# Decoder step on one core: the up-projection's adding DMA is loaded with another weight part, and loads and splits are emitted in turn

## The chip, the core and the metric

The kernel runs on one core of a Trainium2 chip. A time is the device time of one execution in microseconds (us); the figure for a kernel is the median of its runs. A core has five engines with a queue each, which work in their program's order: TensorE (PE; its weight loads are listed as PEld), VectorE (DVE), ScalarE (ACT), GpSimd (POOL) and SyncE (SP). Here SP only issues DMA transfers; POOL issues the adding ones.

## The reference, cut to what matters

One layer of a hybrid decoder for 576 tokens (512 of a prompt, 64 of eight samples), all in float32, with a model width of 1024:

```python
xn = rms_norm(h, g_mix);  z = xn @ w_in                        # 1024 -> 6144
...                                                            # short convolution, pooling, gates
h = h + (gate_a * ya + gate_b * yb) @ w_o
hn = rms_norm(h, g_mlp)
h = h + jnp.square(jax.nn.relu(hn @ w_up)) @ w_down            # 1024 -> 4096 -> 1024
gp = jax.nn.sigmoid(rms_norm(h, g_ple) @ w_ple_gate)
h = h + gp * (p @ w_ple_proj);  y = rms_norm(h, g_final)
```

## The kernel before

Every float32 product is made of three matmuls on float32r parts: a number is split into hi (rounded) and lo (the rest), and hi·hi, hi·lo and lo·hi are added up. So every weight has to be split on the chip. A weight part is 128 x 512 numbers (256 KB). Its way is: SP loads it into one of the 8 buffers `raw` (line 114); ACT writes hi (line 79) and DVE writes lo (line 80) into one of the NF = 7 buffer pairs of `wsp`; PE uses it. A `raw` buffer comes free when the last reader of its part is through, a `wsp` pair when PE is through with it. A new part takes the `raw` buffer that has been free the longest, and its load waits on SP for that buffer's last reader, which is nearly always the lo of an earlier part on DVE.

The list `order` holds all parts in the order of use, and the class `Stream` emits loads and splits ahead of the use: `take` hands out parts and sees to it that splits are emitted up to NF parts beyond the oldest part in use, and loads some parts beyond that. A scheduler then orders each engine's instructions by its own estimates; a load or split emitted earlier does not have to run earlier.

The up-projection `w_up` is done in four blocks (`b`) of 1024 columns, each followed by its block of `w_down`. In a block the columns go in four pairs of 128-column units (`Pair`), and a pair takes seven products instead of eight (Strassen-Winograd: sums of quarter blocks of the weights times sums of quarter blocks of the activations). The weights of a pair are the quarters a, b (of the first unit) and c, d (of the second), and the forms to be multiplied are a, s2 = (c+d)+a, s0 = c+a (up to the signs of the algorithm), s1 = c+d, b, d and s3 = -s2-b:

```python
order += [Form(pairs[0], "a")]
for q in range(NQ):
    order += [Form(pairs[q], n) for n in ("s2", "s0", "s1", "b")]
    if q + 1 < NQ:
        order += [Form(pairs[q + 1], "a")]
    order += [Form(pairs[q], n) for n in ("d", "s3")]
```

Two of these sums are made by the DMA engines: `Pair.summed` loads c by SP and then has POOL issue a DMA from `w_up` that adds d (for s1) or a (for s0) onto the same `raw` tile (line 140); POOL waits for the plain load before it issues. s2 is made from s1's tile and a's tile by DVE (line 160, tile `s`), s3 by DVE too (line 162).

PE multiplies the forms in `quarter` (line 481), twelve matmuls a form. Products share four PSUM tiles `ab` and `cd`, and DVE combines them in between: line 532 (`u`, after the product for s2), line 534 (`g`, after that for s0), line 536 (after that for s1), line 557 at the pair's end. A product that is added onto such a tile waits until DVE has read it. These instructions stand in the same DVE queue as the splits and lines 160 and 162.

Of the kernel before, what the change touches and what calls it, by code (L numbers as in the profile page):

```python
# [42 lines left out]
def tile_hybrid_step(ctx: ExitStack, tc: tile.TileContext, x, pt, vecs, rc, ident, sconv, spool, w_first, w_in,  # L43
# [68 lines left out]
    def raw_tile(ap):  # L112
        raw = wraw.tile([P, KH], F32, tag="raw", name="raw")
        nc.sync.dma_start(raw, ap)
        return raw

    class Part:

        def __init__(self, ap, resident=False):
            self.ap, self.resident = ap, resident  # L120

        def load(self):
            self.raw = raw_tile(self.ap)
# [19 lines left out]
    class Form:  # L143
# [2 lines left out]

        def load(self):
            p, name = self.pair, self.name
            if name in ("a", "b", "d"):
                setattr(p, "r" + name, raw_tile(getattr(p, name)))  # L150
            elif name == "s2":
                p.rs1 = p.summed(p.c, p.d)
            elif name == "s0":
                p.rs0 = p.summed(p.c, p.a)

# [8 lines left out]
            return split(p.rs2 if name == "s3" else getattr(p, "r" + name), [P, KH], wsp, "w")  # L164

    class Stream:
        def __init__(self, items, loads=5):
            self.items, self.loads = items, loads
            self.nload, self.used, self.parts = 0, 0, []

        def fill(self, loads, splits):
            n = len(self.items)
            while self.nload < min(loads, n):
                self.items[self.nload].load()
                self.nload += 1
            while len(self.parts) < min(splits, n):
                self.parts.append(self.items[len(self.parts)].split())

        def take(self, n=1, live=0):

            first = self.used - live
            for i in range(n):
                splits = min(self.used + n + NF - 1, first + NF)
                self.fill(splits + self.loads, splits)
            out = self.parts[self.used:self.used + n]
            for i in range(self.used, self.used + n):
                self.parts[i] = self.items[i] = None
            self.used += n
            return out
# [165 lines left out]
    for j in range(NJ):  # L355
# [16 lines left out]
        n = CEXT - (CW - 1)  # L372
# [398 lines left out]
```

## Time and profile before

| | |
|---|---|
| median of 3 runs | 921.03 us (918.36 to 922.82) |
| the profiled execution | 923.7 us, of which 921.9 us are the span from the first to the last instruction |
| PE busy (matmul) | 898.6 us, 97% of the span |
| DVE, ACT, POOL busy | 521.3, 370.1, 113.4 us |
| weights and data | 89.60 MB read, 2.99 MB written |
| granted TensorE clock, mean | 0.984 of full speed |

PE is busy nearly throughout, so the time is PE's work, the stretches in which it waits, and the stretches in which it is granted half its clock. The blocks of `w_up` run at about 437 to 485 us, 535 to 586 us, 637 to 688 us and 739 to 791 us; they are called blocks 0 to 3.

### The profile page before, as it was taken

The numbers are of one execution on the slowest core, as the hardware profiler recorded it, in microseconds if no ns is written. First come the engines' busy times: TensorE is split into PE (matmuls) and PEld (weight loads), VectorE is DVE, ScalarE is ACT, GpSimd is POOL, SyncE is SP. The second block draws the span as 40 slices with busy tenths as digits, with TensorE's granted clock in tenths as the row PEclk, the third lists the DMA queues.
The fourth block names the chain that finished last, engine by engine and source line by source line (L and its number), as shares of the span: only waits on it lengthen the run. The fifth ranks groups of instructions, "written<-read, shape, count | busy, mean of one in ns | idle before, by whom it ended". The sixth has DMA issues, their size and how long they took to land.

```text
span 921.9 us, 16512 instructions
## 1 busy us (share of the span) xinstructions
PE 898.6 (97%) x6650; PEld 893.6 (97%) x6650; DVE 521.3 (57%) x832; ACT 370.1 (40%) x626; POOL 113.4 (12%) x150
## 2 busy tenths in 40 slices
PE   8999999999999999999999998999899989999995
PEld 7999999999999999999999998999899989999995
DVE  7654444433336687778863246544574356687555
ACT  8222222332113333355674245512472145545532
POOL 5000000000001221022100010010000010021243
PEclk9999999999999999999999999999899998999997
DMA  7422222222222222334544453363443453322102
GB/s 266 140 81 82 89 82 81 84 84 89 81 82 80 86 85 82 105 103 99 155 127 114 105 126 111 94 146 92 124 128 97 105 126 109 99 92 97 31 10 94
DMA packets 52653, 93.66 MB, mean 102 GB/s; under 512 B 6240, under 2 KB 9952, under 8 KB 52576
## 3 DMA queue, kind: packets, MB, share of 16 engines
q1 hardware_dynamic: 47824, 84.18, 28.8%
q0 software_dynamic: 4608, 8.39, 5.8%
q8 instruction: 52, 0.85, 0.4%
q14 instruction: 25, 0.20, 0.1%
q10 hardware_dynamic: 144, 0.03, 0.0%
HBM read 89.60 MB, written 2.99 MB: 100 GB/s over the span
## 4 chain that ended last, share of the span: by engine, by line
PE 92%; DMA 3%; ACT 2%; DVE 2%; issue 1%; POOL 0%; SPq 0%; DVEq 0%; POOLq 0%
PE ps L95 67%; PE cd L481 10%; PE ab L481 7%; PE psg L95 6%; DMA raw<-w_up 2%; PE psf L95 1%; PE psn L323 1%; DVE lo L80 1%; ACT hi L79 1%; ACT hi L82 0%; PE psn L307 0%; POOL sq L298 0%; ACT sq L294 0%; DMA xall<-x 0%; DVE xall L653 0%
## 5 line engine op out<-in xcount | busy, mean ns | idle before, releaser
L79 ACT CAST hi<-raw 128x512 fp32r<-128x512 f32 x290 | 177.8, 619 | 404.7 <-PE ps L95 325.9
L95 PE MATMUL ps<-hi,lo 128*128 128x288 f32 x1552 | 332.7, 296 | 0.0
L95 PE MATMUL ps<-lo,hi 128*128 128x288 f32 x1552 | 332.6, 296 | 0.0
L95 PE MATMUL ps<-hi 128*128 128x288 f32 x1552 | 332.5, 296 | 0.0
L80 DVE TENSOR_TENSOR lo<-raw,hi 128x512 fp32r<-128x512 f32 x290 | 203.7, 710 | 151.9 <-ACT hi L79 150.4
L95 PEld LDWEIGHTS ps<-hi,lo 128*128 128x128 f32 x1552 | 250.2, 189 | 0.0
L95 PEld LDWEIGHTS ps<-hi 128*128 128x128 f32 x1552 | 250.1, 189 | 0.0
L95 PEld LDWEIGHTS ps<-lo,hi 128*128 128x128 f32 x1552 | 250.1, 189 | 0.0
L481 PE MATMUL cd<-hi 128*128 128x288 f32 x256 | 78.2, 306 | 8.8 <-DVE g L534 8.6
L481 PE MATMUL cd<-lo,hi 128*128 128x288 f32 x256 | 77.0, 301 | 1.4 <-DVE lo L80 1.4
L481 PE MATMUL cd<-hi,lo 128*128 128x288 f32 x256 | 77.0, 301 | 0.0
L140 POOL DMA_DIRECT2D raw<-w_up x32 | 27.9, 879 | 330.8 <-DVE lo L80 154.0
L481 PEld LDWEIGHTS cd<-hi 128*128 128x128 f32 x256 | 49.1, 192 | 10.6 <-DVE g L534 9.4
L481 PE MATMUL ab<-hi 128*128 128x288 f32 x192 | 59.1, 308 | 0.0
L298 POOL TENSOR_TENSOR sq<-sq 128x576 f32<-128x576 f32 (+2 forms) x34 | 43.0, 1264 | 126.7 <-ACT sq L294 70.7
L481 PE MATMUL ab<-hi,lo 128*128 128x288 f32 x192 | 58.3, 305 | 0.0
L481 PE MATMUL ab<-lo,hi 128*128 128x288 f32 x192 | 58.1, 302 | 0.0
L481 PEld LDWEIGHTS cd<-lo,hi 128*128 128x128 f32 x256 | 49.4, 193 | 1.6 <-DVE lo L80 1.6
L481 PEld LDWEIGHTS cd<-hi,lo 128*128 128x128 f32 x256 | 49.4, 193 | 0.0
L481 PEld LDWEIGHTS ab<-hi 128*128 128x128 f32 x192 | 37.8, 197 | 1.5 <-ACT g L519 0.7
L95 PE MATMUL psg<-hi 128*128 128x320 f32 (+1 forms) x128 | 38.2, 298 | 0.0
L481 PEld LDWEIGHTS ab<-hi,lo 128*128 128x128 f32 x192 | 37.9, 198 | 0.0
(129 smaller groups left out, 882.4 us busy)
## 6 DMA issues: line engine op xcount, KB each, us to landing
raw<-w_in SPq DMA_DIRECT2D x90, 256.0 KB, 2.7
raw<-w_up SPq DMA_DIRECT2D x80, 256.0 KB, 2.9
raw<-w_down SPq DMA_DIRECT2D x64, 256.0 KB, 2.7
raw<-w_up POOLq DMA_DIRECT2D x32, 256.0 KB, 4.6
raw<-w_oc SPq DMA_DIRECT2D x16, 256.0 KB, 2.7
raw<-w_o SPq DMA_DIRECT2D x16, 256.0 KB, 2.7
raw<-w_pg SPq DMA_DIRECT2D x16, 256.0 KB, 2.8
xall<-x SPq DMA_DIRECT2D x7, 288.0 KB, 5.5
```

The source lines that it names most:

```text
L79: nc.scalar.copy(hi, src)
L80: nc.vector.tensor_tensor(out=lo, in0=src, in1=as32(hi), op=ALU.subtract)
L95: nc.tensor.matmul(o, wt, cols(at), start=start and i == 0, stop=stop and i == 2)
L140: nc.gpsimd.dma_start(raw, y, accum_op=ALU.add)
L298: nc.gpsimd.tensor_tensor(out=self.parts[0], in0=self.parts[0], in1=sq, op=ALU.add)
L323: nc.tensor.matmul(self.ps[:, h, c:c + m], self.y[:, i:i + 1].broadcast_to([m, P]), idt[:m, :m], start=True, stop=True)
L481: nc.tensor.matmul(o, wt, at, start=start and k == 0 and i == 0, stop=stop and k == NQ - 1 and i == 2, skip_group_check=True)
```

## The change

Three things are edited. The stream's number `loads` goes from 5 to 6. `fill` emits a load, a split, a load, a split, where it emitted all loads and then all splits of a call. And the tile of s1, with its plain load and its adding DMA, is loaded together with a of the same pair, where it was loaded with s2; in `order`, a stands three places ahead of s2 (one place in a block's first pair).

```diff
         def load(self):
             p, name = self.pair, self.name
+            if name == "a":
+                p.rs1 = p.summed(p.c, p.d)
             if name in ("a", "b", "d"):
                 setattr(p, "r" + name, raw_tile(getattr(p, name)))
-            elif name == "s2":
-                p.rs1 = p.summed(p.c, p.d)
             elif name == "s0":
                 p.rs0 = p.summed(p.c, p.a)
...
     class Stream:
-        def __init__(self, items, loads=5):
+        def __init__(self, items, loads=6):
...
         def fill(self, loads, splits):
             n = len(self.items)
-            while self.nload < min(loads, n):
-                self.items[self.nload].load()
-                self.nload += 1
+            def load(upto):
+                while self.nload < min(upto, n):
+                    self.items[self.nload].load()
+                    self.nload += 1
+
             while len(self.parts) < min(splits, n):
+                load(len(self.parts) + self.loads)
                 self.parts.append(self.items[len(self.parts)].split())
+            load(loads)
...
             for i in range(n):
                 splits = min(self.used + n + NF - 1, first + NF)
-                self.fill(splits + self.loads, splits)
+                self.fill(0, splits)
```

Lines below `fill` stand four lines further down in the changed kernel (line 534 is line 538 there). Three places show what moved in the programs.

The loads on SP for the third and fourth pair of block 1 (numbers are kept in the names here). Before, `raw_6104` is s1 of the third pair, `raw_6124` its s0, `raw_6162` its b, `raw_6194` a of the fourth pair, `raw_6214` d of the third, `raw_6252` s1 of the fourth, `raw_6272` s0 of the fourth:

```order
L114 DMA raw_6104<-w_up 128x512
L114 DMA raw_6124<-w_up 128x512
L114 DMA raw_6162<-w_up 128x512
L114 DMA raw_6194<-w_up 128x512
L114 DMA raw_6214<-w_up 128x512
L114 DMA raw_6252<-w_up 128x512
L114 DMA raw_6272<-w_up 128x512
```

Now `raw_6069` is d of the second pair, `raw_6124` s0 and `raw_6162` b of the third, and then `raw_6194` is s1 of the fourth, `raw_6197` its a, `raw_6217` d of the third, `raw_6272` s0 of the fourth:

```order
L114 DMA raw_6069<-w_up 128x512
L114 DMA raw_6124<-w_up 128x512
L114 DMA raw_6162<-w_up 128x512
L114 DMA raw_6194<-w_up 128x512
L114 DMA raw_6197<-w_up 128x512
L114 DMA raw_6217<-w_up 128x512
L114 DMA raw_6272<-w_up 128x512
```

The fourth pair's s1 went ahead of its a and of d: two places up on SP, from the buffer that the split of b of the second pair frees to the buffer that the split of s0 of the second pair frees, two splits earlier on DVE. s0 of the fourth pair keeps its place and its buffer's release. Every pair has this swap; outside `w_up` SP's rows and what they wait for are the same in both programs.

DVE at the same place, around line 160 of the fourth pair of block 1 (tile `s2_6362`), before:

```order
L557 TENSOR_TENSOR g_6042<-cd_6044,u_6045 128x2x288
L80 TENSOR_TENSOR lo_6198<-s2_6068,hi_6197 128x512
L532 TENSOR_TENSOR u_6193<-ab_6131,g_6144 128x288
L160 TENSOR_TENSOR s2_6362<-raw_6252,raw_6194 128x512
L80 TENSOR_TENSOR lo_6219<-s2_6216,hi_6218 128x512
L534 TENSOR_TENSOR g_6144<-cd_6192,u_6193 128x288
L162 SCALAR_TENSOR_TENSOR s2_6216<-s2_6216,raw_6162 128x512
L80 TENSOR_TENSOR lo_6236<-raw_6124,hi_6235 128x512
```

And now:

```order
L561 TENSOR_TENSOR g_6042<-cd_6044,u_6045 128x2x288
L80 TENSOR_TENSOR lo_6201<-s2_6071,hi_6200 128x512
L160 TENSOR_TENSOR s2_6362<-raw_6194,raw_6197 128x512
L536 TENSOR_TENSOR u_6193<-ab_6131,g_6144 128x288
L80 TENSOR_TENSOR lo_6222<-s2_6219,hi_6221 128x512
L162 SCALAR_TENSOR_TENSOR s2_6219<-s2_6219,raw_6162 128x512
L538 TENSOR_TENSOR g_6144<-cd_6192,u_6193 128x288
L80 TENSOR_TENSOR lo_6239<-raw_6124,hi_6238 128x512
```

Line 160 now stands ahead of `u` (line 532 before, 536 now), and line 162 ahead of `g` (line 534 before, 538 now). Blocks 2 and 3 have the same rows.

PE at the same place: behind the product for s0 (`cd`) it starts the last one onto `ab` and then that for s1 onto `cd`. Before, from the last matmul for s0 on:

```order
L481 MATMUL cd_6192<-hi_4885,lo_6088 128x288
L481 MATMUL ab_6131<-hi_4416,hi_6127 128x288
L481 MATMUL ab_6131<-lo_4417,hi_6127 128x288
L481 MATMUL ab_6131<-hi_4416,lo_6128 128x288
L481 MATMUL ab_6131<-hi_4416,hi_6127 128x288
L481 MATMUL ab_6131<-lo_4417,hi_6127 128x288
L481 MATMUL cd_6192<-hi_4428,hi_6107 128x288
```

And now:

```order
L485 MATMUL cd_6192<-hi_4885,lo_6091 128x288
L485 MATMUL ab_6131<-hi_4416,hi_6127 128x288
L485 MATMUL ab_6131<-lo_4417,hi_6127 128x288
L485 MATMUL ab_6131<-hi_4416,lo_6128 128x288
L485 MATMUL ab_6131<-hi_4416,hi_6127 128x288
L485 MATMUL ab_6131<-lo_4417,hi_6127 128x288
L485 MATMUL ab_6131<-hi_4416,lo_6128 128x288
L485 MATMUL ab_6131<-hi_4723,hi_6127 128x288
L485 MATMUL ab_6131<-lo_4724,hi_6127 128x288
L485 MATMUL ab_6131<-hi_4723,lo_6128 128x288
L485 MATMUL cd_6192<-hi_4428,hi_6107 128x288
```

Nine matmuls onto `ab` stand ahead of the next one onto `cd`, where there were five. In block 0 the first two instructions of line 160 also moved up on DVE, into the stretch in which `w_o` still runs: that of the first pair now stands ahead of lines 505 to 508 (`Operand.add`) for k = 0, that of the second pair ahead of those for k = 1.

## Rows read from the trace of the kernel before

**Rows 1.** The page: the span, PE's busy time, and the span in 40 equal slices (PEclk is the granted clock in tenths of full speed).

```profile
span 921.9 us, 16512 instructions
PE 898.6 (97%) x6650; PEld 893.6 (97%) x6650; DVE 521.3 (57%) x832; ACT 370.1 (40%) x626; POOL 113.4 (12%) x150
PEclk9999999999999999999999999999899998999997
```

**Rows 2.** Who waited for whom on PE, and on DVE for a DMA, over the whole span: us in total, times, longest us.

```profile
PE cd L481 <- DVE g L534: 8.6, 3, 2.9
PE cd L481 <- DVE lo L80: 1.4, 1, 1.4
...
DVE s L160 <- DMA raw<-w_up: 31.9, 11, 5.4
```

**Rows 3.** Stretches of the span: us, busy us (and instructions) of PE, PEld, DVE, ACT and POOL, then the granted clock, the share of the DMA engines and GB/s. The first three are the stretches at half clock in blocks 1 to 3 in which PE worked, the last is PE's wait at the start of block 0.

```profile
557.02:560.43 3.41, 3.41 (x16) 3.41 (x15) 2.58 (x5) 1.55 (x3) 0.00 (x0) 0.50 0.27 77
657.04:662.83 5.79, 5.79 (x24) 5.79 (x25) 3.95 (x7) 1.55 (x3) 0.00 (x0) 0.50 0.16 45
759.30:765.23 5.93, 5.93 (x25) 5.93 (x26) 4.09 (x7) 1.54 (x3) 0.00 (x0) 0.50 0.15 47
440.33:441.69 1.36, 0.00 (x1) 0.00 (x0) 1.36 (x4) 0.69 (x2) 0.00 (x0) 1.00 1.09 207
```

**Rows 4.** The chain of waits that ended last, in block 1: start us, us, what.

```profile
544.92 0.69 DVE lo L80
...
545.63 3.51 DMA raw<-w_up
...
549.70 4.26 DMA raw<-w_up
...
555.76 2.23 PE cd L481 x12
```

**Rows 5.** DVE's instructions in block 1 in order of time: start us, us, line, operation, out<-in, count, and in brackets the idle time before it and what ended it.

```profile
541.77 0.68 DVE L80 TENSOR_TENSOR lo<-raw,hi 128x512 fp32r<-128x512 f32 x1
...
549.78 0.68 DVE L80 TENSOR_TENSOR lo<-s,hi 128x512 fp32r<-128x512 f32 x1
550.70 0.46 DVE L532 TENSOR_TENSOR u<-ab,g 128x288 f32<-128x288 f32 x1 [0.23 <-PE ab L481]
554.04 0.69 DVE L160 TENSOR_TENSOR s<-raw 128x512 f32<-128x512 f32 x1 [2.89 <-DMA raw<-w_up]
554.65 0.68 DVE L80 TENSOR_TENSOR lo<-s,hi 128x512 fp32r<-128x512 f32 x1
555.25 0.45 DVE L534 TENSOR_TENSOR g<-cd,u 128x288 f32<-128x288 f32 x1
```

**Rows 6.** PE's matmuls around that wait, in the same form.

```profile
552.09 0.29 PE L481 MATMUL ab<-hi 128*128 128x288 f32 x1
552.22 0.29 PE L481 MATMUL ab<-lo,hi 128*128 128x288 f32 x1
...
555.76 0.40 PE L481 MATMUL cd<-hi 128*128 128x288 f32 x1 [2.84 <-DVE g L534]
...
557.31 0.44 PE L481 MATMUL cd<-lo,hi 128*128 128x288 f32 x1
557.55 0.44 PE L481 MATMUL cd<-hi,lo 128*128 128x288 f32 x1
```

**Rows 7.** DVE in blocks 2 and 3, the places that answer to 541.77 and 550.70 of block 1.

```profile
642.95 0.68 DVE L80 TENSOR_TENSOR lo<-raw,hi 128x512 fp32r<-128x512 f32 x1
...
651.88 0.46 DVE L532 TENSOR_TENSOR u<-ab,g 128x288 f32<-128x288 f32 x1 [0.23 <-PE ab L481]
...
745.28 0.68 DVE L80 TENSOR_TENSOR lo<-raw,hi 128x512 fp32r<-128x512 f32 x1
...
754.21 0.46 DVE L532 TENSOR_TENSOR u<-ab,g 128x288 f32<-128x288 f32 x1 [0.23 <-PE ab L481]
```

**Rows 8.** Issues of DMA transfers and their time to landing: first that of all 32 adding ones (line 140, issued by POOL), then the plain load that SP issued at 542.5 us and the one at 643.7 us, each with its issue (min, median and max ns, first and last start).

```profile
DMA to landing us min/median/max: 3.9/4.6/6.0
...
L114 SPq DMA_DIRECT2D raw<-w_up x1: 327/327/327, 542.5 to 542.5; - x1
...
DMA to landing us min/median/max: 3.3/3.3/3.3
...
L114 SPq DMA_DIRECT2D raw<-w_up x1: 327/327/327, 643.7 to 643.7; - x1
...
DMA to landing us min/median/max: 2.6/2.6/2.6
```

**Rows 9.** DVE while `w_o` runs, ahead of block 0, in the form of rows 5.

```profile
405.42 0.68 DVE L80 TENSOR_TENSOR lo<-raw,hi 128x512 fp32r<-128x512 f32 x1
...
410.23 0.68 DVE L80 TENSOR_TENSOR lo<-raw,hi 128x512 fp32r<-128x512 f32 x1
411.16 0.76 DVE L505 TENSOR_TENSOR gt<-gx 128x576 f32<-128x576 f32 x1 [0.24 <-ACT gx L573]
...
418.66 0.69 DVE L160 TENSOR_TENSOR s<-raw 128x512 f32<-128x512 f32 x1 [0.46 <-DMA raw<-w_up]
...
432.86 1.57 DVE L80 TENSOR_TENSOR lo<-raw,hi 128x512 fp32r<-128x512 f32 x1 [1.39 <-ACT hi L79]
435.16 0.76 DVE L570 TENSOR_TENSOR xall<-ps,xall 128x576 f32<-128x576 f32 x1 [0.72 <-PE ps L95]
```

## The prediction, made before the changed kernel was run

> **What bounds the kernel now.** The page comes first: PE is busy 97% of a span of 921.9 us [rows 1], so only two things can be won without taking work away from PE, the stretches in which it waits and those in which its clock is halved. The waits of PE over the whole span show one that matters: three times, 8.6 us together, at most 2.9 us each, a matmul onto `cd` waited for line 534 of DVE; next comes a single one of 1.4 us [rows 2]. The row of clock digits dips between 550 and 790 us [rows 1], and the table of stretches says where: behind each of the three waits PE worked at half clock, for 3.41, 5.79 and 5.93 us [rows 3]. The fourth stretch of that table is a wait of 1.36 us, and the clock stayed at 1.00.
>
> Who made line 534 late? DVE in order of time shows it for block 1: `u` is done at 551.2, then line 160 of the fourth pair starts at 554.04 after 2.89 us of waiting for a DMA, and line 534, two places behind it, runs at 555.25 and ends at 555.70; PE goes on at 555.76 [rows 5, 6]. The chain of waits goes further back: DVE's split at 544.92 frees a `raw` buffer, the plain load into it is issued at 545.63 and lands 3.51 us later, POOL issues the adding DMA at 549.70, and that lands after 4.26 us, at 553.96 [rows 4]. So PE waits for s1 of the fourth pair, because its transfer has a chain of two DMAs behind a buffer that comes free too late, and because the reader of that tile stands in front of line 534 in an in-order queue. Most waits of line 160 are not felt by PE: they come to 31.9 us in 11 places [rows 2].
>
> **The change, part by part.** *Six instead of five, and loads in turn with splits.* Before, a call that emits one split first emitted loads up to five parts beyond that split's end; now the load six places on from the split's own place is emitted just before it. For a call of one part that is the same load; for calls of two parts the second load comes one split later. The programs bear this out: outside `w_up` no load on SP changed its place or what it waits for. When a load starts is set by its buffer's release. I put these two edits at 0 us; nothing has to hide them.
>
> *s1 with its adding DMA at a's place.* It adds and removes no instruction: the same plain loads, 32 adding DMAs, splits and matmuls. What moves is two issues in every pair, the plain load and POOL's. In block 1 the fourth pair's s1 takes the buffer that is free after DVE's split at 541.77 + 0.68 = 542.45 [rows 5], not 544.92 + 0.69 = 545.61 [rows 4]. SP has nothing queued ahead of it then: a load was issued at just that time, 542.5, and landed after 3.3 us [rows 8]. POOL issued 0.56 us behind the landing (549.70 against 545.63 + 3.51) [rows 4], and an adding DMA lands 4.6 us after its issue in the median [rows 8]. Sum: 542.5 + 3.3 + 0.56 + 4.6 = 551.0, instead of 553.96. Pushed back by this are a and d, one plain load each; a is read by the same line 160 and now waits for a split that ended at about 545, lands at about 548 and so is not the last. s0 keeps its place, and its adding DMA follows s1's at a greater distance than now.
>
> *The new order on DVE and PE.* Line 160 starts at the later of 551.0 and the time DVE is through with what stands ahead of it, 549.78 + 0.68 = 550.46 [rows 5]. From there to the end of `g` stand line 160 (0.61 us from start to start), `u` (0.46 us, 0.1 us of it overlapped), a lo (0.60), line 162 (of the same size, 0.60) and `g` itself (0.45) [rows 5]: 2.6 us, so `g` ends at 553.6. PE has nine matmuls onto `ab` ahead of the one that needs `g`, and one takes 0.133 us (552.09, 552.22) [rows 6]: it arrives at 552.09 + 9 x 0.133 = 553.3. That leaves a wait of some 0.4 us in block 1. In block 2 the split that frees the buffer ends at 643.63 [rows 7], the load of that time landed after 2.6 us [rows 8], so s1 is complete at 643.7 + 2.6 + 0.56 + 4.6 = 651.4; DVE is free at 651.88 - 0.23 = 651.65 [rows 7], `g` ends at 654.3, and PE arrives at 553.3 + (651.88 - 550.70) = 654.5. No wait; block 3 has the same distances (745.96 and 754.21 [rows 7]). So of 8.6 us of waiting 8.2 go.
>
> *The clock.* At half clock a matmul takes 0.24 us (557.31, 557.55) against 0.133 [rows 6], so a stretch loses 45% of itself: 3.41, 5.79 and 5.93 us [rows 3] give 1.5 + 2.6 + 2.6 = 6.7 us. The clock fell behind waits of 2.8 to 2.9 us and not behind one of 1.36 us [rows 2, 3], and what I leave is 0.4 us, so I take the 6.7 us as won.
>
> *Block 0.* Two instructions of line 160 now stand ahead of lines 505 to 508 while `w_o` runs. That of the second pair stood at 418.66; now it stands behind the lo at 410.23 [rows 9], and its s1 takes the buffer of the split that ended at 405.42 + 0.68 = 406.10 [rows 9], about 1 us later now because the first pair's line 160 waits ahead of it; with 3, 0.56 and 4.6 us it is complete at about 415, so DVE stands still for about 4 us there and lines 505 onwards start near 416 instead of 411.16. What hides it is DVE's slack: the 0.46 us wait and the 0.69 us of line 160 at 418.66 fall away, and up to 435.16 there are idle times of 1.39 and 0.72 us before rows that wait for PE's pace [rows 9], with smaller ones between. I take 0; uncovered, it is up to 0.9 us more on PE's wait at 440.33.
>
> **The sum.** 8.6 - 0.4 + 6.7 = 14.9 us, on the profiled execution 923.7 - 14.9 = 908.8 (span 907.0). That execution lies 2.7 us over the median of the runs, 921.03, so I predict 921.03 - 14.9 = **906.1 us**.
>
> **The bounds.** The unknown is how long the adding DMA takes at its new time. The rows go from 3.9 to 6.0 us [rows 8]. At 3.9 no wait is left in any block, and the gain is 15.3 us. At 6.0 the waits are 1.8, 1.2 and 1.2 us, 11.1 us are won with the clock and 4.4 without it, since 1.8 us lies between the wait that left the clock alone and those that did not. I take 4.6, the median, because the DMA at the new place has no other adding DMA beside it.
>
> [...]
>
> **The rivals.** *Forecast:* the three waits are gone but for at most about 1 us in all, the clock stays up; 904 to 908.5 us. Chance 0.70.
>
> *The adding DMA is slower where it now lies.* Between 545 and 549 us SP issues four more plain loads, and the adding DMA is now in flight with them. For it: the spread of 3.9 to 6.0 us. Against: adding DMAs had plain loads beside them before too, and the median is 4.6. Waits of 1 to 2 us stay, and in some blocks the clock falls: 908.5 to 914. Chance 0.14.
>
> *Block 0 starts later.* DVE's 4 us are not made up by 435; PE's 1.36 us become up to 2.3 us, and if the clock falls there, 2.6 us more: 907 to 910. Chance 0.06.
>
> *The change doesn't do what it says.* Line 160 waits for something else, a's load or POOL's turn, and `g` is as late as now; 917 to 922. Against: both were seen to be earlier above. Chance 0.06.
>
> *Slower.* Line 160 stands ahead of `u` now, and two more instructions lie between it and `g`, so a late DMA holds up more than before. With the adding DMA landing x after 551.0, PE waits 0.4 + x; it waits as long as now at an adding DMA of 7.0 us, and to lose 4.6 us over three blocks it takes 8.5 us. No row is above 6.0 [rows 8]; over 925.6. Chance 0.04.
>
> **How the numbers follow.** About 0.5% (4.6 us) is what a measurement of this kernel can tell from no change. Faster by more than that, under 916.4: 0.70 + 0.14 + 0.06 = 0.90; within it 0.06; slower 0.04. For eight in ten the range takes the forecast, block 0 and the better half of the slow DMAs: 903.5 to 913, with the lower end below the 905.7 of a gain of 15.3 us because three runs of the kernel before spread from 918.36 to 922.82.
>
> **What would show it.** Right: no `cd <- g` wait above 0.6 us among PE's waits; clock 1.00 in blocks 1 to 3; a DVE wait of line 160 in the fourth pair under 1 us, with the adding DMA issued about 3 us earlier against line 534; blocks 1 to 3 each some 4 to 5 us shorter than their 51 us. Wrong: line 160 waits 2 us or more there, or PE waits for `u`, or the first wait of block 0 has grown past 2 us, or the mean clock stays near 0.984.

## The result and the profile after

The changed kernel takes 914.78 us in the median of 18 runs (913.1 to 919.04), beside it the kernel before 919.84 us (18 runs): a ratio of 0.9938, 95% interval 0.9918 to 0.9958. It is faster by 0.6%, some 5.7 us by the ratio (the medians differ by 5.1). The forecast was 906.1 us, the range ended at 913.0: the direction was right, the size about two fifths of what was forecast. (Ratios leave out executions that were disturbed as a whole.)

The profiled execution of the changed kernel takes 914.79 us. Its page, beside [rows 1]: the span is 8.9 us shorter, and the row of clock digits no longer dips between 550 and 790 us.

```profile
span 913.0 us, 16513 instructions
PE 894.4 (98%) x6650; PEld 888.9 (97%) x6650; DVE 519.7 (57%) x832; ACT 369.8 (41%) x626; POOL 114.0 (12%) x150
PEclk9999999999999999999999999999999999999998
```

Who waited for whom on PE, beside [rows 2] (us in total, times, longest):

```profile
PE ab L485 <- ACT hi L79: 2.7, 1, 2.7
PE ab L485 <- DVE u L536: 2.2, 3, 1.2
...
PE cd L485 <- DVE g L538: 0.7, 3, 0.2
PE cd L485 <- DVE lo L80: 0.5, 1, 0.5
```

The three waits for `g`, 8.6 us, have become 0.7 us, but three waits for `u` of 2.2 us together are new, and the wait at the start of block 0, once 1.36 us [rows 3], is 2.7 + 0.5 us. The third place to look is DVE in block 1 (start, us, line, operation, in brackets the idle time), beside [rows 5]:

```profile
545.03 0.68 DVE L80 TENSOR_TENSOR lo<-raw,hi 128x512 fp32r<-128x512 f32 x1
...
553.04 0.68 DVE L80 TENSOR_TENSOR lo<-s,hi 128x512 fp32r<-128x512 f32 x1
555.57 0.69 DVE L160 TENSOR_TENSOR s<-raw 128x512 f32<-128x512 f32 x1 [1.85 <-issue]
556.18 0.45 DVE L536 TENSOR_TENSOR u<-ab,g 128x288 f32<-128x288 f32 x1
...
557.87 0.45 DVE L538 TENSOR_TENSOR g<-cd,u 128x288 f32<-128x288 f32 x1
```

The split that frees the buffer starts at 545.03, where it stood at 541.77: this execution reaches block 1 3.26 us later than that of before (block 0, below). From there the chain runs as forecast until the adding DMA, which is issued at 549.5 us and lands after 6.0 us, at 555.49; line 160 starts right behind it (the profile names no releaser for its 1.85 us), and `u`, which now stands behind line 160, is late. The issue of that DMA, and those of blocks 2 and 3 (min, median, max; start; then the time to landing):

```profile
L140 POOL DMA_DIRECT2D raw<-w_up x1: 862/862/862, 549.5 to 549.5; - x1
...
DMA to landing us min/median/max: 6.0/6.0/6.0
...
L140 POOL DMA_DIRECT2D raw<-w_up x1: 862/862/862, 647.5 to 647.5; - x1
...
DMA to landing us min/median/max: 5.7/5.7/5.7
...
L140 POOL DMA_DIRECT2D raw<-w_up x1: 865/865/865, 745.3 to 745.3; - x1
...
DMA to landing us min/median/max: 6.0/6.0/6.0
```

The four plain loads that SP issues at 548.3 to 552.0 us, in flight with the first of these, are slowed as well: 4.4 us in the median, where two of before took 3.3 and 2.6 us [rows 8]:

```profile
L114 SPq DMA_DIRECT2D raw<-w_up x4: 327/328/922, 548.3 to 552.0; - x4
...
DMA to landing us min/median/max: 2.7/4.4/5.3
```

PE sees it as 1.18 us for `u` and 0.23 us for `g`, and keeps its clock:

```profile
556.68 0.40 PE L485 MATMUL ab<-hi 128*128 128x288 f32 x1 [1.18 <-DVE u L536]
...
558.38 0.40 PE L485 MATMUL cd<-hi 128*128 128x288 f32 x1 [0.23 <-DVE g L538]
```

### The profile page after: what moved, and what is told of

The parts are those of the page before. It is cut to its first block, busy times and chain, and to the rows that moved or that the text cites. A ratio compares the mean times of both kernels' runs of the same rounds, so it can differ in the third digit from the quotient of the medians.

```text
span 913.0 us, 16513 instructions
## 1 busy us (share of the span) xinstructions
PE 894.4 (98%) x6650; PEld 888.9 (97%) x6650; DVE 519.7 (57%) x832; ACT 369.8 (41%) x626; POOL 114.0 (12%) x150
## 4 chain that ended last, share of the span: by engine, by line
PE 89%; DVE 3%; DMA 3%; issue 2%; ACT 2%; POOL 0%; SPq 0%; DVEq 0%; POOLq 0%; ACTq 0%
PE ps L95 65%; PE cd L485 10%; PE ab L485 7%; PE psg L95 6%; DMA raw<-w_up 3%; DVE lo L80 1%; PE psf L95 1%; PE psn L327 1%; ACT hi L79 1%; ACT sq L298 1%; POOL sq L302 0%; PE psn L311 0%; ACT hi L82 0%; DMA xall<-x 0%; DVE xall L574 0%
## 5 line engine op out<-in xcount | busy, mean ns | idle before, releaser
L95 PE MATMUL psg<-lo,hi 128*128 128x320 f32 (+1 forms) x128 | 37.9, 296 | 0.0
```

The costliest lines, as they stand in the source:

```text
L95: nc.tensor.matmul(o, wt, cols(at), start=start and i == 0, stop=stop and i == 2)
```

## The experiments

Line numbers differ by a few between the kernels: the sum of line 160 is line 161 or 163 in those below, `u` is line 537, 540 or 541, and PE's products are line 486, 489 or 490.

**The first two edits alone, and the third alone.** The kernel before with the first two edits:

```diff
-        def __init__(self, items, loads=5):
+        def __init__(self, items, loads=6):
...
                 load(len(self.parts) + self.loads)
                 self.parts.append(self.items[len(self.parts)].split())
```

> Only the first two edits: six parts ahead instead of five, loads and splits in turn; s1 stays with s2. Every engine's instructions and what each waits for are those of the kernel before, so the time must be that of the kernel before, 919.8 us, within its scatter. What the run tells apart is how typical the profiled execution of the kernel before was. Theory 'the clock dips are a fixed part of it': the three waits for g of 2.8 to 2.9 us come again, and behind each of them PE works 3.4 to 5.9 us at half clock, 15.1 us in all, mean clock 0.984. Rival 'the dips come and go between executions': the three waits are the same, but the stretches at half clock are fewer or shorter, and the mean clock is 0.986 to 0.992.

Measured: 919.43 us, ratio 1.0008 (0.9987 to 1.003): no difference, as it must be. What it shows is the clock. Its waits for `g` are those of before, its mean clock 0.992 instead of 0.984, its span 916.0 us instead of 921.9:

```profile
PE cd L485 <- DVE g L538: 8.2, 3, 3.0
```

```profile
556.16 0.40 PE L485 MATMUL cd<-hi 128*128 128x288 f32 x1 [3.00 <-DVE g L538]
...
657.14 0.40 PE L485 MATMUL cd<-hi 128*128 128x288 f32 x1 [2.64 <-DVE g L538]
...
756.58 0.40 PE L485 MATMUL cd<-hi 128*128 128x288 f32 x1 [2.58 <-DVE g L538]
```

The stretches behind these three waits (the granted clock stands ahead of the last two columns):

```profile
556.76:560.17 3.41, 3.41 (x17) 3.41 (x16) 2.42 (x5) 0.62 (x1) 0.00 (x0) 0.50 0.25 77
657.14:663.97 6.83, 6.83 (x51) 6.83 (x52) 5.13 (x9) 3.09 (x6) 0.00 (x0) 1.00 0.36 119
756.58:763.41 6.83, 6.83 (x51) 6.83 (x52) 5.14 (x9) 3.09 (x6) 0.00 (x0) 1.00 0.38 116
```

Half the clock behind the first, all of it behind the other two, where the profiled execution of before worked 5.79 and 5.93 us at half clock [rows 3]. PE's instructions and their order are the same in both programs, so the rival holds: the dips come and go between executions. Over 17 executions of the kernel before that ran beside this one the mean clock was 0.983 to 0.993, 0.990 in the median; the one execution that the forecast was read from, at 0.984, lay at the low end. The 18 of the changed kernel had 0.987 to 0.996, median 0.992. Two things limit what this mean can tell. It counts half clock outside the four blocks too: in the traces here a stretch near 24 us of the span, which is missing or 3.41 or 6.83 us long, and the last 6 to 11 us. And two of the 36 executions of the kernel before whose clock is on record (909.03 us at 0.992, 915.07 us at 0.983) were some 8 to 10 us faster than others at the same or nearly the same clock; there is no trace of them, so the reason is open.

The third edit alone was run later, with two kernels below, and gives the changed kernel's ratio again, so the first two edits are worth nothing: 913.53 us, ratio 0.9929 (0.9908 to 0.995), with 2.0 + 0.7 us of waits for `u` and `g`, and for block 0 1.2 + 1.7 us without a fall of the clock.

> Only the third edit: s1 is loaded with a, with the old five parts ahead and all loads of a call ahead of its splits. Every engine's instructions and waits are those of the changed kernel, so the first two edits are worth nothing if the time is the changed kernel's, 914.8 us within its scatter (ratio 0.992 to 0.996). It is the yardstick for the other two kernels on this chip. For block 0: PE's first wait is 2.4 to 2.9 us again; whether the clock falls behind it is open, 1.5 us for each 3.41 us at half clock.

**Are the plain loads what slows the adding DMA?** The changed kernel, with transfers in flight beside the fourth pair's s1 cut to an eighth of their columns in blocks 1 to 3: three of the four plain loads (d, c for s0 and b; a stays whole) and s0's adding DMA. So this kernel leaves out seven eighths of these weights.

```diff
-        nc.sync.dma_start(raw, ap)
+        nc.sync.dma_start(raw[:, :n], ap[:, :n])
+        if n < KH:
+            nc.gpsimd.memset(raw[:, n:], 0.0)
...
+                      {2: ("d",), 3: ("s0", "b")}.get(q, ()) if b else ()) for q in range(NQ)]
```

> The changed kernel, but in blocks 1 to 3 the plain loads that were in flight with the adding DMA of the fourth pair's s1 (d of the third pair, c for s0 and b of the fourth) and s0's adding DMA move an eighth of their columns; POOL fills the rest with zeros, so these weights are wrong. Theory 'the adding DMA is slow because it shares the DMA engines with those loads': issue to landing of the fourth pair's s1 falls from 5.7 to 6.0 us to 4.0 to 4.6, line 160 starts some 1.3 us earlier, and PE's waits for u of 1.18, 0.40 and 0.66 us are gone. Rival 'an adding DMA of this size is that slow here by itself': it stays at 5.5 us or more, and the waits stay.

Measured (a single execution, 909.53 us): the three DMAs land after 4.0, 4.7 and 4.3 us; PE has no wait for `u` or `g` at all. That of block 1, and DVE behind it:

```profile
L143 POOL DMA_DIRECT2D raw<-w_up x1: 862/862/862, 548.4 to 548.4; - x1
...
DMA to landing us min/median/max: 4.0/4.0/4.0
```

```profile
551.85 0.68 DVE L80 TENSOR_TENSOR lo<-s,hi 128x512 fp32r<-128x512 f32 x1
552.56 0.69 DVE L163 TENSOR_TENSOR s<-raw 128x512 f32<-128x512 f32 x1
553.17 0.45 DVE L540 TENSOR_TENSOR u<-ab,g 128x288 f32<-128x288 f32 x1
```

Line 163, the sum, follows the split without a gap. The contention is shown (5.7 to 6.0 us against 4.0 to 4.7), and it is what made the new wait. It doesn't always fall on the same transfer. In the four traces with s1 at a's place and whole loads the adding DMA took 4.7 to 6.2 us in blocks 1 to 3; where it took 4.7 and 4.8 us (block 1 with the third edit alone, and with block 0 put back, below) the plain load ahead of it took 4.0 and 3.8 us instead of 3.2, POOL issued 0.9 and 0.7 us later against DVE's split, and PE still waited 0.8 and 0.6 us for `u`. The table of stretches says that the DMA engines were not busier than before, but moved more. The first row is the changed kernel from issue to landing in block 1, the second this one, the third the kernel before:

```profile
549.47:555.49 6.02, 6.02 (x46) 5.80 (x44) 2.74 (x4) 4.06 (x8) 0.86 (x1) 1.00 0.78 206
```

```profile
548.35:552.38 4.03, 4.03 (x32) 4.03 (x32) 2.60 (x4) 2.07 (x6) 2.23 (x4) 1.00 0.68 140
```

```profile
549.70:553.96 4.26, 3.21 (x25) 2.98 (x23) 1.22 (x3) 4.06 (x7) 1.74 (x2) 1.00 0.79 142
```

**Earlier still.** If contention and landing are all, an s1 that lands earlier, ahead of those loads, must end the waits. s1 of the next pair is loaded with b of this one (in blocks 1 to 3, where a block's first pair keeps s1 with its a; block 0 as before the change):

```diff
...
+            if name == "b" and p.after and p.after.early:
+                p.after.rs1 = p.summed(p.after.c, p.after.d)
```

> As the kernel with block 0 put back, but in blocks 1 to 3 the s1 of the second to fourth pair is loaded one form earlier still, with b of the pair before, so that it takes the buffer that DVE frees at 540.9 and not at 545.7 in block 1. Theory 'what is left in blocks 1 to 3 is the landing of s1': the fourth pair's adding DMA lands by 550, even at 6 us, line 160 waits for it no longer, PE's waits for u (1.18, 0.40, 0.66 us) are gone, 2.2 us less than with block 0 put back alone: 909 us. Rival 'the waits are made by the order on DVE, two more instructions ahead of g': PE still waits 0.2 to 1.2 us in each block, and the time is that of the kernel with block 0 put back. A second rival: b, which now comes behind, lands too late for line 162, and g waits for that: PE waits 1 us or more for g in each block.

Measured: 908.74 us, ratio 0.9876 (0.9854 to 0.9898), no wait for `u` or `g`, the three DMAs at 3.9 to 4.0 us. The order on DVE and PE is the changed kernel's there, so that order costs nothing once s1 lands in time, and b behind it is not late.

Is it these three transfers alone? The next kernel moves only them (`early` for `b > 0 and q == 3`), everything else stays as before the change:

> Only three transfers are moved: in blocks 1 to 3 the fourth pair's s1 is loaded with b of the third pair; every other pair, and all of block 0, loads s1 with s2 as the kernel before does. Theory 'the waits for g are made by that one transfer of each block alone': the three waits of 2.7 to 3.0 us for g are gone as in the kernel with all pairs moved, and the time is that one's, 908.7 us (ratio 0.9876 to before), within 1 us. Rival 'the first three pairs matter too': they gain or lose by the move, and the time is 1.5 us or more away from 908.7.

Measured: 908.02 us (907.31 to 909.26), ratio 0.9846 (0.9794 to 0.9899): yes, the other pairs neither gain nor lose by more than the scatter (the two kernels ran on different chips, with medians of 918.5 and 920.87 us for the kernel before). Its DMA in block 1 and DVE behind it, where line 163 has no idle time ahead of it:

```profile
L141 POOL DMA_DIRECT2D raw<-w_up x1: 865/865/865, 540.5 to 540.5; - x1
...
DMA to landing us min/median/max: 3.9/3.9/3.9
```

```profile
549.69 0.68 DVE L80 TENSOR_TENSOR lo<-s,hi 128x512 fp32r<-128x512 f32 x1
550.41 0.69 DVE L163 TENSOR_TENSOR s<-raw 128x512 f32<-128x512 f32 x1
551.01 0.45 DVE L541 TENSOR_TENSOR u<-ab,g 128x288 f32<-128x288 f32 x1
```

One step more, with s0 of the pair before, brings nothing: 908.78 us, ratio 0.9856 (0.9804 to 0.9908), and one wait for `g` of 0.4 us.

> As the kernel of 908.7 us (block 0 left alone), but s1 is loaded two forms earlier still, with s0 of the pair before, so it holds a buffer for longer and b and a come behind it. Theory 'once s1 lands in time, earlier brings nothing more': no waits for u or g in blocks 1 to 3 and 908.7 us within 1 us. Rival 'a buffer held longer makes another load the late one': line 162 or 160 waits for b's or a's load, PE waits 1 us or more in each of blocks 1 to 3, and the time is 912 us or more.

**Block 0.** In the changed kernel DVE runs up to block 0 like this, beside [rows 9]:

```profile
410.51 0.67 DVE L80 TENSOR_TENSOR lo<-raw,hi 128x512 fp32r<-128x512 f32 x1
415.95 0.69 DVE L160 TENSOR_TENSOR s<-raw 128x512 f32<-128x512 f32 x1 [4.77 <-DMA raw<-w_up]
...
436.58 1.58 DVE L80 TENSOR_TENSOR lo<-raw,hi 128x512 fp32r<-128x512 f32 x1 [1.39 <-ACT hi L79]
438.08 0.74 DVE L574 TENSOR_TENSOR xall<-ps,xall 128x576 f32<-128x576 f32 x1
```

and PE, with the stretch at half clock that begins 0.57 us before the end of its first wait:

```profile
440.82 0.61 PE L485 MATMUL ab<-hi 128*128 128x288 f32 x1 [2.66 <-ACT hi L79]
...
444.94 0.40 PE L485 MATMUL cd<-lo,hi 128*128 128x288 f32 x1 [0.47 <-DVE lo L80]
```

```profile
440.25:443.66 3.41, 2.84 (x12) 2.84 (x13) 3.38 (x5) 2.05 (x4) 2.10 (x2) 0.50 0.67 191
```

DVE stands 4.77 us for the second pair's s1, and the last `xall` of `w_o`, which had waited 0.72 us for PE at 435.16 [rows 9], starts at 438.08 with no idle time: of 4.8 us some 2.9 reach the start of block 0. The third edit alone shows the same with a shorter stop: 3.25 us, of which 1.3 reach the last `xall` (436.49), and 1.16 us PE's first wait:

```profile
414.34 0.69 DVE L160 TENSOR_TENSOR s<-raw 128x512 f32<-128x512 f32 x1 [3.25 <-DMA raw<-w_up]
...
436.49 0.75 DVE L570 TENSOR_TENSOR xall<-ps,xall 128x576 f32<-128x576 f32 x1
```

With s1 loaded with s2 in block 0 alone:

```diff
+            if name == ("a" if p.early else "s2"):
+                p.rs1 = p.summed(p.c, p.d)
...
+        pairs = [Pair(w_up[b * NJ + q], w_up[b * NJ + NQ + q], b > 0) for q in range(NQ)]
```

> The changed kernel, but in block 0 s1 is loaded with s2 again; blocks 1 to 3 as in the changed kernel. Theory 'the two instructions of line 160 that moved up into w_o cost block 0 its time': PE's wait at the start of block 0 is 1.4 us again instead of 2.66, the one of 0.47 us behind it is gone, no stretch at half clock there (3.41 us, a loss of 1.5 us), so 3.3 us less than the changed kernel: 911.5 us. Rival 'block 0 is late for another reason, the changed transfers of w_o's last weights': the wait stays at 2.4 us or more and the time within 1 us of the changed kernel's 914.8. Blocks 1 to 3 keep their 2.9 us of waits in either case.

Measured: 913.63 us, ratio 0.9929 (0.9907 to 0.9952), 2.1 us over what was expected. By its time alone that can't be told from the changed kernel. The wait of 2.66 us became one of 1.74 us, but the clock fell behind it all the same:

```profile
442.34 0.40 PE L486 MATMUL ab<-lo,hi 128*128 128x288 f32 x1 [1.74 <-DVE lo L80]
```

```profile
443.29:446.70 3.41, 3.41 (x16) 3.41 (x16) 3.09 (x6) 1.59 (x4) 0.00 (x0) 0.50 0.28 90
```

An estimate that takes the clock out speaks for a cost of block 0: each execution's time less 45% of its time at half clock, 2 x (1 - mean clock) x time, gives medians of 909.1 us for the changed kernel, 906.7 for this one, 908.6 for the third edit alone and 906.7 for the same without block 0 and the first three pairs (below). The mean clock has three digits, so each execution is good to 0.4 us at best, and the four didn't all run on one chip.

The other way round, with block 0 made early in the kernel of 908.7 us, the answer is clearer:

> s1 of the second to fourth pair is loaded with b of the pair before in all four blocks, block 0 too, so that the two early instructions of line 160 in w_o are back; blocks 1 to 3 as in the kernel of 908.7 us. Theory 'the early line 160 costs block 0 its time whatever lands when': PE waits 2.4 to 3 us at the start of block 0 (1.5 where block 0 is left alone) and the time is 1 to 3 us above 908.7. Rival 'it was the late landing of the second pair's s1, and earlier is early enough': DVE's stop at about 411 to 416 us shrinks to under 2 us, PE's wait is 1.7 us or less, and the time is that of 908.7 within 0.7 us.

Measured: 909.94 us (909.51 to 910.68), ratio 0.9864 (0.9802 to 0.9926), 1.9 us over the median of the kernel with three moved transfers, which ran on the same chip, and each of its four runs over each of that one's (the two differ in the first three pairs of blocks 1 to 3 as well, which made no difference above). PE's waits in block 0 are two here and one there:

```profile
441.54 0.40 PE L490 MATMUL ab<-hi 128*128 128x288 f32 x1 [1.53 <-ACT hi L79]
445.50 0.40 PE L490 MATMUL cd<-lo,hi 128*128 128x288 f32 x1 [1.55 <-DVE lo L80]
```

```profile
441.62 0.40 PE L490 MATMUL cd<-lo,hi 128*128 128x288 f32 x1 [1.40 <-DVE lo L80]
```

3.1 us against 1.4: the first theory. DVE's idle time ahead of the second pair's sum is only 1.07 us here, but the split ahead of it takes 2.62 us instead of 0.68:

```profile
412.21 2.62 DVE L80 TENSOR_TENSOR lo<-raw,hi 128x512 fp32r<-128x512 f32 x1
415.90 0.78 DVE L163 TENSOR_TENSOR s<-raw 128x512 f32<-128x512 f32 x1 [1.07 <-DMA raw<-w_up]
...
438.80 0.74 DVE L579 TENSOR_TENSOR xall<-ps,xall 128x576 f32<-128x576 f32 x1
```

What PE sees is how late DVE is at the last `xall`. From the `xall` that starts at 397 to 399 us to the last one DVE takes 38.40 us before the change and with three moved transfers, 41.19 us in the changed kernel, 39.70 with the third edit alone and 40.06 here, so it is 2.8, 1.3 and 1.7 us late, and PE's first wait is 2.66, 1.16 and 1.53 us. Why that split takes so long is open, and so is what the second wait of PE, 0.47 to 1.7 us, owes to the move.

**The parts on one chip.** The move for the three transfers alone, with a as in the change, and the same with b, beside the third edit alone (913.53 us, above):

> The move of the change for three transfers alone: in blocks 1 to 3 the fourth pair's s1 is loaded with its a; every other pair and block 0 as in the kernel before. Theory 'the change is worth what the landing of these three gives, and block 0 takes part of it back': adding DMAs of 5 to 6 us beside the plain loads, 2 to 3 us of waits for u and g left, block 0's wait 1.4 us; 1.5 to 3 us less than the changed kernel and 2 to 4 us more than with b in the place of a. Rival 'block 0 takes nothing back': the changed kernel's time within 1 us.

Measured: 911.3 us (910.38 to 913.71), ratio 0.9904 (0.9882 to 0.9927), 2.0 + 0.7 us of waits for `u` and `g` and 1.5 us in block 0.

> The kernel of 908.0 us once more, on the chip of the two others: those three transfers one form earlier, with b of the third pair. No waits for u or g, adding DMAs of 3.9 to 4.1 us; 908 us, ratio to before 0.984 to 0.989. If it is less than 4 us under the changed kernel, the order of what was found is wrong.

Measured: 908.94 us (907.54 to 910.45), ratio 0.9876 (0.9855 to 0.9897), 4.6 us under the third edit alone. The adding DMAs took 4.2 to 4.3 us, a little over the 3.9 to 4.1 expected, and PE has no wait for `u` or `g`. So on one chip: 919.72 us before; the change, by its third edit, 913.5; without its moves in block 0 and in the first three pairs 911.3, with the same 2.7 us of waits for `u` and `g`; with s1 ahead of the other loads 908.9. This last kernel beats both.

## Why the forecast was right in direction and wrong in size

**What bounds the kernel**, the chain of two DMAs behind a buffer and line 160 ahead of `g`: right, and shown by the kernel that moves three transfers of the program, ends all three waits and is 10.8 us under the kernel before.

**The first two edits at 0 us:** right (ratio 1.0008).

**The adding DMA at 4.6 us:** the first step that failed. Buffer release, plain load and POOL's issue came as forecast: 545.03 + 0.68 = 545.71 to an issue at 549.47 is 3.76 us, forecast 3.3 + 0.56 = 3.86. Then 6.02, 5.74 and 5.98 us instead of 4.6. The reason given for the median, no other adding DMA beside it, looked at the wrong neighbours: in the kernel before POOL issued another one 0.9 us behind it, at 550.6, and it took 4.26 us all the same [rows 4]. In these runs the plain loads decide: with three of the four cut to an eighth it takes 4.0 to 4.7 us. The waits left are 0.7 + 2.2 = 2.9 us instead of 0.4, so 2.5 us are missing here. The bounds held: at 6.0 us the text had 1.8, 1.2 and 1.2 us (its own times give 1.0 and 0.9 for the last two), the trace has 1.4, 0.6 and 0.9. The rival of an adding DMA that is slower where it now lies (0.14) had named the four plain loads in flight with it: in block 1 the adding DMA of POOL took 6.0 us beside four plain loads of SP and 4.0 us with three of them cut to an eighth.

**The order on DVE and PE:** right in its parts. From line 160 to the end of `g` it takes 558.32 - 555.57 = 2.75 us, forecast 2.6. But PE's wait shows at `u`, which the text did not place in its sum, though it named a wait for `u` as a sign that it was wrong.

**Block 0 at 0 us:** the second step that failed. The stop was forecast well (about 4 us up to 416; 4.77 us up to 415.95), its cover was not: the idle times counted as slack were mostly waits that return in the changed kernel (1.39 us ahead of a split, there too), and only some 1.9 us were truly free (4.77 - 2.9, and 3.25 - 1.3 with the third edit alone). The wait grew from 1.36 to 3.1 us, by 1.8 us, and the clock fell behind it in this execution.

**The clock at 6.7 us:** the third, and the largest. Its rate is right: the spans of before and of the first two edits alone differ by 5.9 us, and 15.1 against 3.41 us at half clock make 5.3 of that, the waits for `g` 0.4. That the 15.1 us belong to the kernel was read from one execution, and the one with the first two edits alone, in which PE has the same instructions and waits as often for `g` (8.2 us), had 3.41 us there. By the medians of the mean clock, 0.990 and 0.992, the change wins 2 x 0.002 x 919 = 3.7 us at half clock, 45% of it 1.7 us (an estimate, since the clock has three digits). That execution lay 2.7 us over the median, which the text saw, and took the whole gain off the median all the same. So 5.0 us are missing.

Together: 14.9 - 2.5 - 1.8 - 5.0 = 5.6 us, and 5.7 were measured. The clock in block 0, up to 1.5 us (45% of the 3.41 us at half clock), is in the mean clock already. That the sum meets the measurement so closely is luck: over all 36 executions of the kernel before whose clock is on record the median is 0.989, by which the clock's term is 2.5 us and the sum 6.4. The kernel with the three transfers loaded with b bears out the size: it ends the 8.6 us of waits, leaves block 0 alone and wins 10.8 us on the last chip, so about 2 us are left for the clock (an estimate).

**What of the other rivals:** "block 0 starts later" (0.06) came true beside that of the slower adding DMA; each was priced alone, block 0 with the clock's 6.7 us won and the slow DMA with only a part of them lost, and so both ended at or below 914. "Doesn't do what it says" and "slower" are out: PE's wait in a block fell from 2.8 or 2.9 us to 1.4 at most, and the order alone costs nothing.

## What to carry to other kernels

Price a transfer that is moved by what will be in flight with it at its new time (here 5.7 to 6.0 us beside four plain loads, 3.9 to 4.3 us ahead of them), not by the median of its kind (4.6), and move it past that crowd if it can go earlier. DVE's stop was hidden here only by idle time that did not return when everything was shifted, 1.9 of 4.77 us: follow such an engine's last instruction ahead of the consumer, not the sum of its gaps. And before a dip of the clock is counted as won, ask whether other executions have it (here 15.1 us at half clock in blocks 1 to 3 in one, 3.41 us in another with the same instructions on PE); an execution above the median may owe that to the dips.

## What the runs showed of the hardware that was not expected

An adding DMA of 256 KB took 3.9 to 4.3 us ahead of the crowd and 5.7 to 6.0 us in the changed kernel with four plain loads beside it, while the busy share of the DMA engines over the first of these was the same as before (0.78 and 0.79) and the rate higher (206 against 142 GB/s).

No length of a single wait of PE separates the dips of the clock seen here: none behind 2.64 and 2.58 us, one behind 3.00, one behind 2.66 in the changed kernel, one behind 1.74 with block 0 put back. In blocks 1 to 3 alone a length would fit: the clock fell behind the waits for `g` of 2.84 us and more in the kernel before and of 3.00 us with the first two edits, and not behind 2.64 and 2.58. The waits differ a little between executions, then, and the clock fell behind all three in one execution and behind one in another. No kernel was run that shifts a wait alone, so what decides it stays open.
